# HGRN mixer of a two-block network: two heads on the rows, both directions in the free dimension

## The chip, the cores and the metric

The kernel runs on one core of one Trainium2 chip. The metric is the time of one execution on the device in microseconds; the kernel before takes 1346.8 us (median of 3 runs, 1343.59 to 1347.79). TensorE multiplies matrices, VectorE, ScalarE and GpSimd work elementwise, and SyncE issues most DMAs. The five run side by side and wait for each other by semaphores.

## The reference

The network has a first block (dilated attention, a gated recurrence, cross attention, an MLP) and a second one of two layers, with 256 tokens of 1024 features. Each layer of the second block normalizes, projects into four mixers (latent attention, FNet, differential attention, HGRN2), gates and sums their outputs, and ends with a SwiGLU. The change is in HGRN2, four heads with keys and values of 64 features, run forward and backward:

```python
def forget(z, lb):
    f = lbh + (1.0 - lbh) * sigmoid(z)          # [b, s, head, 64]
    return 1.0 - f, log(f)
k_f, lf_f = forget(f_fwd_in, lb_fwd)
k_b, lf_b = forget(f_bwd_in, lb_bwd)
o_fwd = hgrn2_chunk_scan(q, k_f, v, lf_f)
o_bwd = flip(hgrn2_chunk_scan(flip(q), flip(k_b), flip(v), flip(lf_b)))
o = rmsnorm(o_fwd + o_bwd, g_on) * sigmoid(g_in)
# hgrn2_chunk_scan, per head: out[t] = sum over s <= t of
#   sum_d q[t,d] * exp(lf[s+1..t, d] summed) * k[s,d] * v[s]
```

So each pair of a query and a key has a weight in which every feature is decayed by the gates of all tokens between the two.

## The kernel before

All weights are streamed once, in blocks of 8 tiles of 128 x 128. A block is split into a high part on ScalarE (`_split`, L365, tile `whi`) and a low part on VectorE (L367, `wlo`), and each product of a weight tile with activations is three TensorE instructions, high by high, high by low, low by high (`mm3`, L391 to L393, output `pl`). These products of the layer's input are called the ordinary products here; `lin_t` (L603 to L605) is their form with 512 columns. Mixers are Python generators. `drive` emits one step of each mixer that has started behind each pair of chunks of ordinary products, and a scheduler, with the priorities of `urgent`, then sets the order on each engine. That order is fixed when the program is built; each engine works through its own.

HGRN (`hgrn`, L1342 on) works with a tree over the 256 tokens instead of a scan. The rows of its tiles are 64 features of the forward gates and 64 of the backward gates; heads and tokens lie along the free dimension. `hk` holds keys and `hq` queries, both times decays to the border of the current block; `tot` holds the decay of whole blocks. For each of 7 levels, with blocks of 1, 2, 4 to 64 tokens, the kernel does the following. GpSimd (L1365) writes `qz`, the queries with those rows and halves zeroed that must not meet at this level: the second halves of block pairs stay for forward rows, the first for backward rows. TensorE multiplies the keys of each head and token tile by `qz` (L1371, 8 products, 128 rows, 128 columns, tile `ph`). In fp32 each is two instructions, called passes here. VectorE copies the results into the score matrix `at` where a mask says so (L1374, twice). Then it multiplies the decays into keys (L1383) and queries (L1384) and forms the totals of blocks of twice the size (L1386), each once for the forward and once for the backward rows. The next level's products need these. The diagonal (L1352, `pd`) is computed ahead of the levels, and the products between the two token tiles (L1393, 64 rows) behind them; outputs follow (L1403, L1404).

Other places that are spoken of: dilated attention's scores have 64 rows per head (L1064, `sc`), its outputs 64 columns (L1075); differential attention splits its operands on VectorE, stacks them by DMA (`dks`) and multiplies (L1456, `sd`); sums over partitions for norms are products with 1 to 4 columns (L435).

Of the kernel before, what the change touches and what calls it, by code (L numbers as in the profile page):

```python
# [9 lines left out]
F32 = mybir.dt.float32  # L10
# [9 lines left out]
T = 256  # L20
# [35 lines left out]
def _forget_cols():  # L56
    """Per head the forward and the backward gate's 64 columns."""
    f, b = _cols("hff").reshape(4, 64), _cols("hfb").reshape(4, 64)
    return np.stack([f, b], 1).reshape(-1)


# [6 lines left out]
def plan():  # L68
    """The streamed weights in the order in which they are used: (array, index, columns, kind)."""
# [21 lines left out]
    for l in range(LAYERS):  # L91
        f("w_in_2", (l,), _forget_cols())
# [34 lines left out]
class Cols:  # L127
    """Columns of a [128, n] array, by name."""
# [24 lines left out]
def mla_rows(odd):  # L153
    """Features of a query in the rows of its operand: the plain ones and the rotated ones, those twice."""
    plain = np.arange(64)
    a, b = 64 + np.arange(16), 80 + np.arange(16)
    return np.concatenate([a, b, b, a, plain] if odd else [plain, a, b, b, a])


def params(inp):  # L160
# [27 lines left out]
    lb = np.asarray(inp["hgrn_lb_logits_2"]).reshape(2, 2, 4, 64)  # [dir, layer, head, 64]  # L188
    c.add("lb", lb.transpose(0, 3, 1, 2))                          # [(dir, 64), layer, head]
# [12 lines left out]
def gate_blocks(inp):  # L202
    a = [np.asarray(inp[n])[0].reshape(2, 4, 2, 64, 64) for n in ("rg_a_w", "rg_x_w")]
    a = np.stack(a, 0)                                             # [g, dir, chunk, half, i, j]
    return np.ascontiguousarray(a.transpose(3, 4, 0, 1, 2, 5)).reshape(2, 64, 16, 64)


def constants():
# [17 lines left out]
    c.add("halves", halves())  # L226
# [20 lines left out]
    an = (np.arange(T, dtype=f32)[:, None] * inv2[None]).astype(f32).astype(f8).T      # [16, 256]  # L247
# [10 lines left out]
def masks():  # L258
    """Pairs (key, query) of one 128-token tile whose blocks of 2^l tokens are the halves of one block of 2^(l+1)."""
    s = np.arange(128)  # L260
    m = np.zeros((128, 7, 128))
    for li in range(7):
        b = 1 << li
        m[:, li] = (s[:, None] // (2 * b) == s[None] // (2 * b)) & (s[:, None] // b != s[None] // b)
    return m.reshape(128, 7 * 128)


def halves():
    """For blocks of 2^l: rows of the forward gates keep the second half, rows of the backward gates the first."""
    z = []  # L270
    for li in range(7):
        b = 1 << li
        f = np.concatenate([np.zeros(b), np.ones(b)])
        z.append(np.concatenate([np.tile(f, (64, 1)), np.tile(1 - f, (64, 1))], 0))
    return np.concatenate(z, 1)


# ---------------------------------------------------------------- device
# [5 lines left out]
class Kern:  # L284
    def __init__(self, ctx, tc, a, pcols, ccols, depth=5, ahead=2):
# [18 lines left out]
        # tiles split at a time: first four, later more  # L304
# [9 lines left out]
    # ---- memory  # L314
# [23 lines left out]
    # ---- weight stream  # L338
    def _dma(self):
# [3 lines left out]
        if self.nd < 32 // TB:  # L343
            # the first blocks and the activations take turns
# [43 lines left out]
    # ---- products  # L388
# [6 lines left out]
    def split(self, hi, lo, src, scale=1.0):  # L395
        """hi + lo = src * scale, both with 12 bits or fewer of mantissa."""
# [34 lines left out]
    def token_sums(self, ps, squares):  # L431
        """ps [128, 2, n] += sums over the partitions of squares, a list of ([p, T], indicator [p, n])."""
# [6 lines left out]
class Norm:  # L439
    """Running sum of squares of a [128, 8, T] tensor, two chunks at a time; then 1/rms."""  # L440
# [6 lines left out]
    def square(self, src, scale=None):  # L447
        """Squares of one or two further chunks, src [128, 1 or 2, T]; added behind the next products."""
# [16 lines left out]
    def add(self, sq):  # L465
        """sq [128, 2, T] squares"""
# [10 lines left out]
    def sums(self):  # L477
        """psum [128 tokens, 2] sums of the squares of all features"""
# [19 lines left out]
def interleave(filler, gens):  # L498
    """One step of the filler, then one of each of the others, until all are done."""
# [13 lines left out]
def urgent(tc, gen, offset):  # L513
    """Steps of gen, ahead of what was emitted shortly before."""
# [7 lines left out]
class Body(Kern):  # L522
# [91 lines left out]
    def drive(self, items):  # L614
        """Products in order; behind each pair of chunks one step of every mixer that was started."""
# [1169 lines left out]
```

## Time and profile before

| | us |
|---|---|
| median of 3 runs | 1346.8 |
| lowest, highest | 1343.59, 1347.79 |
| span of the profiled execution, first to last instruction | 1341.6 |
| TensorE busy (PE) | 1291.5 |
| TensorE weight loads busy (PEld) | 1243.3 |
| VectorE busy (DVE) | 929.6 |
| ScalarE busy (ACT) | 639.0 |
| GpSimd busy (POOL) | 258.9 |

The profile is of one execution. Spans of TensorE instructions overlap, since products are pipelined: its pace is read from starts, not from lengths. The granted clock is the share of TensorE's full clock (2.4 GHz) that it was given; 0.5 is 1.2 GHz. Time in which an engine is idle costs something only if a later end depends on it.

### The profile page before, as it was taken

To read this page: it belongs to the slowest core of one execution; us is meant where nothing else is said; L and a number is where in the kernel's file an instruction comes from. 1 tells how busy PE (TensorE), PEld (TensorE's weight loads), DVE (VectorE), ACT (ScalarE), POOL (GpSimd) and SP (SyncE) were. 2 spreads that over 40 slices of the span, in tenths; PEclk is the share of its full clock that TensorE was granted. 3 is DMA by queue.
4 is the path that set the end of the run, shared out by engine and by line. 5 is a ranking of instruction groups with operands and counts; after the bars stand their busy time and mean duration, and the time that the engine had idled before them with its cause. 6 is when DMAs were issued, how large, how long until landed. Compare 5 with 4: busy or idle time off the path is not lost. (4 is left out here: it accounts for less than half of the span.)

```text
span 1341.6 us, 24772 instructions
## 1 busy us (share of the span) xinstructions
PE 1291.5 (96%) x10082; PEld 1243.3 (93%) x10082; DVE 929.6 (69%) x1323; ACT 639.0 (48%) x959; POOL 258.9 (19%) x209
## 2 busy tenths in 40 slices
PE   7979999999999889999999999999899999999998
PEld 6867879999999888999999999998789999999998
DVE  6998547665569996756766666589966577666653
ACT  5556446554444226444554444442364545544432
POOL 8675111000013331222010000113312220100000
PEclk9989999999999999999999999999998999999999
DMA  7533445565674353346556566544532455565562
GB/s 271 175 118 95 141 126 159 187 181 181 188 236 150 119 181 95 94 143 178 183 173 184 180 204 221 183 143 124 173 115 65 142 185 176 176 184 188 178 199 64
DMA packets 68610, 216.64 MB, mean 161 GB/s; under 512 B 10376, under 2 KB 16008, under 8 KB 68496
## 3 DMA queue, kind: packets, MB, share of 16 engines
q1 hardware_dynamic: 68448, 215.02, 51.1%
q8 instruction: 79, 1.29, 0.4%
q14 instruction: 35, 0.29, 0.1%
q0 software_dynamic: 48, 0.03, 0.0%
HBM read 208.73 MB, written 1.05 MB: 156 GB/s over the span
## 5 line engine op out<-in xcount | busy, mean ns | idle before, releaser
L367 DVE TENSOR_TENSOR wlo<-w,whi 128x1024 fp32r<-128x1024 f32 (+1 forms) x381 | 489.5, 1288 | 267.5 <-ACT whi L365 265.3
L365 ACT ACTIVATE whi<-w 128x1024 fp32r<-128x1024 f32 (+1 forms) x386 | 403.6, 1050 | 506.9 <-PE pl L392 256.4
L393 PE MATMUL pl<-xh,wlo 128*128 128x256 f32 x1872 | 535.2, 286 | 10.4 <-POOL wlo L367 6.1
L392 PE MATMUL pl<-xl,whi 128*128 128x256 f32 x1872 | 535.8, 287 | 2.9 <-DVE xl L402 2.9
L391 PE MATMUL pl<-xh,whi 128*128 128x256 f32 x1872 | 535.6, 287 | 2.1 <-DVE ckv L1484 0.9
L393 PEld LDWEIGHTS pl<-xh,wlo 128*128 128x128 f32 x1872 | 362.5, 194 | 13.1 <-POOL wlo L367 6.3
L392 PEld LDWEIGHTS pl<-xl,whi 128*128 128x128 f32 x1872 | 362.6, 194 | 5.6 <-DVE xl L402 3.8
L391 PEld LDWEIGHTS pl<-xh,whi 128*128 128x128 f32 x1872 | 362.2, 194 | 5.2 <-issue 1.8
L472 POOL TENSOR_TENSOR sq<-sq 128x512 f32<-128x512 f32 x24 | 33.9, 1416 | 499.2 <-DVE xl L402 284.3
L391 PE MATMUL pl<-fh,whi 128*128 128x256 f32 x352 | 99.7, 283 | 0.5 <-DVE rs L1733 0.5
L392 PE MATMUL pl<-fl,whi 128*128 128x256 f32 x352 | 99.6, 283 | 0.0
L393 PE MATMUL pl<-fh,wlo 128*128 128x256 f32 x352 | 99.6, 283 | 0.0
L391 PE MATMUL pl<-hdh,whi 128*128 128x256 f32 x256 | 72.5, 283 | 0.6 <-DVE rs L1120 0.6
L392 PE MATMUL pl<-hdl,whi 128*128 128x256 f32 x256 | 72.4, 283 | 0.0
L393 PE MATMUL pl<-hdh,wlo 128*128 128x256 f32 x256 | 72.4, 283 | 0.0
L391 PEld LDWEIGHTS pl<-fh,whi 128*128 128x128 f32 x352 | 67.6, 192 | 0.7 <-DVE rs L1733 0.7
L393 PEld LDWEIGHTS pl<-fh,wlo 128*128 128x128 f32 x352 | 67.6, 192 | 0.0
L392 PEld LDWEIGHTS pl<-fl,whi 128*128 128x128 f32 x352 | 67.6, 192 | 0.0
L663 POOL TENSOR_TENSOR p<-p,rd 128x512 f32<-128x512 f32 x28 | 33.5, 1197 | 119.1 <-DVE rd L656 56.1
L391 PEld LDWEIGHTS pl<-hdh,whi 128*128 128x128 f32 x256 | 49.1, 192 | 0.8 <-issue 0.8
L392 PEld LDWEIGHTS pl<-hdl,whi 128*128 128x128 f32 x256 | 49.1, 192 | 0.0
L393 PEld LDWEIGHTS pl<-hdh,wlo 128*128 128x128 f32 x256 | 49.1, 192 | 0.0
(428 smaller groups left out, 2059.3 us busy)
## 6 DMA issues: line engine op xcount, KB each, us to landing
w<-in_W_dram SPq DMA_DIRECT2D x378, 512.0 KB, 3.6
w<-in_W_dram SPq DMA_DIRECT2D x8, 256.0 KB, 4.5
sw<-in_S_dram SPq DMA_DIRECT2D x4, 512.0 KB, 5.4
h<-in_xT_dram SPq DMA_DIRECT2D x8, 128.0 KB, 4.2
mem<-in_memT_dram SPq DMA_DIRECT2D x2, 512.0 KB, 5.8
sw<-qe SPq DMA_DIRECT2D x16, 64.0 KB, 3.2
dt<-in_C_dram SPq DMA_DIRECT2D x4, 256.0 KB, 7.1
dqs<-dhi SPq DMA_DIRECT2D x16, 64.0 KB, 3.5
```

Source lines behind the costliest of these rows:

```text
L365: self.nc.scalar.activation(hi, w, AF.Copy)
L367: eng.tensor_tensor(lo, w, hi.bitcast(F32), op=OP.subtract)
L391: mm(out, wh, xh, start=first, stop=False, skip_group_check=shared)
L392: mm(out, wh, xl, start=False, stop=False, skip_group_check=shared)
L393: mm(out, wl, xh, start=False, stop=last, skip_group_check=shared)
L472: self.eng.tensor_tensor(self.acc, self.acc, sq, op=OP.add)
L663: self.nc.gpsimd.tensor_tensor(p, p, r.rearrange("p (q o) -> p q o", o=1).to_broadcast([128, 2, T]), op=OP.mult)
```

## The change

The rows of the HGRN tiles are now 64 features of one head and 64 of another, and the four places along the free dimension are the two directions of the two head pairs. So the forget gates are projected in two parts, forward and backward, each directly in the layout of its columns; queries come out of their projection in the layout in which they are used, and are one tile of half the size. At each level the products are made per direction, per head and per token tile: 16 instead of 8 products, with 64 rows instead of 128, and with only those 64 queries that meet keys at this level, so that nothing has to be zeroed. The two heads are alternated in the innermost loop and write to two PSUM banks. The masked copies are four instead of two, each for half of the queries. A level's key decays, query decays and totals are one VectorE instruction each, over both directions and all rows, by access patterns written out in `view`. The diagonal takes the sum of forward and backward keys (`ks`). The constant `halves` is gone, and comments are dropped.

```diff
 def plan():
-        f("w_in_2", (l,), _forget_cols())
+        f("w_in_2", (l,), _cols("hff"))
+        f("w_in_2", (l,), _cols("hfb"))
...
 def params(inp):
-    lb = np.asarray(inp["hgrn_lb_logits_2"]).reshape(2, 2, 4, 64)  # [dir, layer, head, 64]
-    c.add("lb", lb.transpose(0, 3, 1, 2))                          # [(dir, 64), layer, head]
+    lb = np.asarray(inp["hgrn_lb_logits_2"]).reshape(2, 2, 2, 2, 64)
+    c.add("lb", lb.transpose(3, 4, 1, 0, 2))
...
 def constants():
-    c.add("halves", halves())
...
 def masks():
-    s = np.arange(128)
-    m = np.zeros((128, 7, 128))
+    s, t = np.arange(128)[:, None], np.arange(128)
+    m = np.zeros((128, 2, 7, 64))
     for li in range(7):
         b = 1 << li
-        m[:, li] = (s[:, None] // (2 * b) == s[None] // (2 * b)) & (s[:, None] // b != s[None] // b)
-    return m.reshape(128, 7 * 128)
+        for z in range(2):
+            q = t[(t // b) % 2 == 1 - z][None]
+            m[:, z, li] = (s // (2 * b) == q // (2 * b)) & ((s // b) % 2 == z)
+    return m.reshape(128, 2 * 7 * 64)
...
-        q0 = self.g4("q0")
+        q0 = self.h2("q0")
...
         def c_hq(j, ps, n):
-            for r in range(2):
-                for par in range(2):
-                    V.tensor_tensor(q0[64 * r:64 * r + 64, par::2], ps[64 * par:64 * par + 64],
-                                    rx["b"][64 * par:64 * par + 64].rearrange("p (o t) -> p o t", o=1)
-                                    .to_broadcast([64, 2, T]), op=OP.mult)
+            V.tensor_tensor(q0, ps, self.bT(rx["b"]), op=OP.mult)
...
         def hgrn():
             ad, ao = at
-            V.tensor_tensor(hq, q0, fz, op=OP.mult)
+            rows = [slice(0, 64), slice(64, 128)]
+            tile = [slice(0, 128), slice(128, 256)]
+            ks = self.h2("ks")
+            V.tensor_tensor(ks, hk[:, 0:2], hk[:, 2:4], op=OP.add)
+            pairs = lambda a: a.rearrange("p (z c) t -> p z (c t)", z=2)
+            V.tensor_tensor(pairs(hq), q0.rearrange("p (o c) t -> p o (c t)", o=1).to_broadcast([128, 2, 512]),
+                            pairs(fz), op=OP.mult)
             yield
+            pd = [self.ps("pd").rearrange("p (k t) -> p k t", k=4) for _ in range(2)]
+            for k in range(4):
+                for p in range(2):
+                    nc.tensor.matmul(pd[p][:, k], ks[rows[p], k // 2, tile[k % 2]], q0[rows[p], k // 2, tile[k % 2]],
+                                     start=True, stop=True)
...
             for li in range(7):
                 B = 1 << li
-                nb = 512 // B                     # pairs of blocks over the heads
-                qz = self.g4("qz")
-                zm = hz[:, 2 * B - 2:4 * B - 2].rearrange("p (o b) -> p o b", o=1).to_broadcast([128, nb, 2 * B])
-                nc.gpsimd.tensor_tensor(qz.rearrange("p h (n b) -> p (h n) b", b=2 * B),
-                                        hq.rearrange("p h (n b) -> p (h n) b", b=2 * B), zm, op=OP.mult)
-                for hp in range(2):
-                    ps = self.ps("ph").rearrange("p (k t) -> p k t", k=4)
-                    for k in range(4):
-                        s = slice((k % 2) * 128, (k % 2) * 128 + 128)
-                        nc.tensor.matmul(ps[:, k], hk[:, 2 * hp + k // 2, s], qz[:, 2 * hp + k // 2, s],
-                                         start=True, stop=True)
-                    m = self.mk[:, li * 128:li * 128 + 128].rearrange("p (o t) -> p o t", o=1)
-                    V.copy_predicated(ad[:, 4 * hp:4 * hp + 4], m.to_broadcast([128, 4, 128]), ps)
-                # decays to blocks of twice the size
-                for z in range(2):
-                    r = slice(64 * z, 64 * z + 64)
-                    tt = tot[z].rearrange("p (n s) -> p n s", s=2)
-                    far, near = tt[:, :, z], tt[:, :, 1 - z]
-                    kh = hk[r].rearrange("p h (n s b) -> p (h n) s b", s=2, b=B)[:, :, z]
-                    qh = hq[r].rearrange("p h (n s b) -> p (h n) s b", s=2, b=B)[:, :, 1 - z]
-                    ex = lambda a: a.rearrange("p (n o) -> p n o", o=1).to_broadcast([64, nb, B])
-                    V.tensor_tensor(kh, kh, ex(near), op=OP.mult)
-                    V.tensor_tensor(qh, qh, ex(far), op=OP.mult)
-                    nt = tots[li % 2][r, :nb]
-                    V.tensor_tensor(nt, far, near, op=OP.mult)
-                    tot[z] = nt
+                nb = 256 // B
+                ps = [self.ps("ph").rearrange("p (z k t) -> p z k t", z=2, k=4) for _ in range(2)]
+                for k in range(4):
+                    c, kt = divmod(k, 2)
+                    for z in range(2):
+                        for p in range(2):
+                            q = hq[rows[p], 2 * z + c, tile[kt]].rearrange("p (n s b) -> p n s b", s=2, b=B)
+                            nc.tensor.matmul(ps[p][:, z, k].rearrange("p (n b) -> p n b", b=B),
+                                             hk[rows[p], 2 * z + c, tile[kt]], q[:, :, 1 - z], start=True, stop=True)
+                for p in range(2):
+                    o = ad[:, 4 * p:4 * p + 4].rearrange("p k (n s b) -> p k n s b", s=2, b=B)
+                    for z in range(2):
+                        m = mk[:, z:z + 1, li].rearrange("p o (n b) -> p o n b", b=B)
+                        V.copy_predicated(o[:, :, :, 1 - z], m.to_broadcast([128, 4, 64 // B, B]),
+                                          ps[p][:, z].rearrange("p k (n b) -> p k n b", b=B))
+                def view(a, o, d, *rest):
+                    return bass.AP(tensor=a.tensor, offset=a.offset + o, ap=[list(a.ap[0]), [d, 2], *rest])
+                first = lambda a: view(a, 0, 512 + B, [2 * B, nb], [1, B])
+                second = lambda a: view(a, B, 512 - B, [2 * B, nb], [1, B])
+                kh, qh = first(hk), second(hq)
+                V.tensor_tensor(kh, kh, view(tot, 1, 2 * nb - 1, [2, nb], [0, B]), op=OP.mult)
+                V.tensor_tensor(qh, qh, view(tot, 0, 2 * nb + 1, [2, nb], [0, B]), op=OP.mult)
+                if li < 6:
+                    tt = tot.rearrange("p (n s) -> p n s", s=2)
+                    nt = tots[li % 2][:, :2 * nb]
+                    V.tensor_tensor(nt, tt[:, :, 0], tt[:, :, 1], op=OP.mult)
+                    tot = nt
                 yield
...
         items = [
-            self.lin(k2, L, 4, x, c_forget), self.lin_t(k2, L, 256, x, c_fx), ...
+            self.lin(k2, L, 2, x, c_forget(0)), self.lin(k2, L, 2, x, c_forget(1)), self.lin_t(k2, L, 256, x, c_fx), ...
```


The order that the scheduler makes of it is known ahead of a run. On TensorE, the products of level 0 in the first of the two layers stood before as one block (`pl` is the ordinary product, `ph` the level's):

```order
L392 MATMUL pl_4814<-xl_84,whi_4778 128x256
L393 MATMUL pl_4814<-xh_83,wlo_4779 128x256
L1371 MATMUL ph_4959<-qz_4957,hk_4411 128x128 x4
L1371 MATMUL ph_4965<-qz_4957,hk_4411 128x128 x4
L391 MATMUL pl_4814<-xh_83,whi_4778 128x256
```

Now the same place begins so, and goes on in this alternation for all 16:

```order
L379 MATMUL pl_4813<-xl_84,whi_4745 128x256
L1360 MATMUL ph_4956<-hq_4412,hk_4411 128x64
L380 MATMUL pl_4813<-xh_83,wlo_4746 128x256
L1360 MATMUL ph_4957<-hq_4412,hk_4411 128x64
L378 MATMUL pl_4813<-xh_83,whi_4745 128x256
```

Each level product has moved between two ordinary products; the second layer has the same pattern. Levels 1 to 6 stand as blocks of 16, alternating the two banks, except that in levels 2 and 4 of both layers 8 or fewer products of another mixer stand ahead of the last one.

On VectorE, the same level stood so before, from the query decays of level 0 on (`wlo` is a weight split, `hgt` and `dqe` are evacuations):

```order
L1384 TENSOR_TENSOR hq_4412<-hq_4412,fz_4410 64x512 x2
L367 TENSOR_TENSOR wlo_4899<-w_4746,whi_4898 128x1024
L1374 COPY_PREDICATED at0_4416<-mk_82,ph_4959 128x512
L1374 COPY_PREDICATED at0_4416<-mk_82,ph_4965 128x512
L1383 TENSOR_TENSOR hk_4411<-hk_4411,fz_4410 64x512 x2
L1307 TENSOR_TENSOR dqe_4420<-pl_4814,n45b_4578 128x512
L1384 TENSOR_TENSOR hq_4412<-hq_4412,tot0_4418 64x256x2 x2
```

Now:

```order
L1324 TENSOR_TENSOR hgt_4414<-pl_4742,n45b_4578 128x512
L1366 COPY_PREDICATED at0_4416<-mk_82,ph_4956 128x256 x2
L1366 COPY_PREDICATED at0_4416<-mk_82,ph_4957 128x256 x2
L1376 TENSOR_TENSOR hk_4411<-hk_4411,fz_4410 128x2x256
L1377 TENSOR_TENSOR hq_4412<-hq_4412,fz_4410 128x2x256
L354 TENSOR_TENSOR wlo_4898<-w_4743,whi_4897 128x1024
L1294 TENSOR_TENSOR dqe_4420<-pl_4813,n45b_4578 128x512
L354 TENSOR_TENSOR wlo_4928<-w_4773,whi_4927 128x1024
```

The four copies, keys and queries follow each other directly, and the weight split that stood between them has moved behind.

## Rows read from the trace of the kernel before

**Rows 1.** The page, part 1: each engine's busy time and instructions.
```profile
PE 1291.5 (96%) x10082; PEld 1243.3 (93%) x10082; DVE 929.6 (69%) x1323; ACT 639.0 (48%) x959; POOL 258.9 (19%) x209
```

**Rows 2.** Windows of HGRN; columns: window, length, PE, PEld, DVE, ACT, POOL, clock, DMA.
```profile
427.60:515.00 87.40, 79.92 (x600) 76.42 (x598) 84.99 (x121) 31.65 (x48) 29.93 (x12) 0.96 0.49 151
...
895.50:983.00 87.50, 80.08 (x598) 76.56 (x598) 84.23 (x118) 32.80 (x48) 30.44 (x12) 0.96 0.47 145
```

**Rows 3.** Waits of TensorE, 400 to 1020 us: total, times, longest.
```profile
PE ph L1371 <- DVE hk L1383: 7.1, 5, 2.2
...
PE sd L1456 <- DMA dks<-dlo: 4.4, 2, 2.3
```

**Rows 4.** Groups by line, level work: busy, mean ns, idle before.
```profile
L1365 POOL TENSOR_TENSOR qz<-hq,ct 128x1024 f32<-128x1024 f32 x14 | 38.3, 2733 | 52.9 <-DVE hq L1384 37.0 <-DVE hq L1345 7.7 <-DVE tot L1386 4.7
...
L1374 DVE COPY_PREDICATED at<-mk,ph 128x512 f32<-128x512 uint8 x28 | 19.5, 730 | 0.1
...
L1383 DVE TENSOR_TENSOR hk<-hk,tot 64x512 f32<-64x512 f32 x24 | 21.6, 901 | 0.3
...
L1384 DVE TENSOR_TENSOR hq<-hq,tot 64x512 f32<-64x512 f32 x24 | 16.4, 682 | 0.4
...
L1386 DVE TENSOR_TENSOR tot<-tot 64x256 f32<-64x256 f32 (+5 forms) x24 | 7.4, 307 | 0.4
```

**Rows 5.** Timeline of GpSimd and VectorE: start, length, instruction.
```profile
445.58 3.20 POOL L1365 TENSOR_TENSOR qz<-hq,ct 128x1024 f32<-128x1024 f32 x1 [3.45 <-PE ph L1371]
...
446.61 3.25 DVE L367 TENSOR_TENSOR wlo<-w,whi 128x1024 fp32r<-128x1024 f32 x1
...
466.67 1.22 DVE L367 TENSOR_TENSOR wlo<-w,whi 128x1024 fp32r<-128x1024 f32 x1
```

**Rows 6.** Timeline of TensorE around a block of level products.
```profile
465.42 0.28 PE L391 MATMUL pl<-xh,whi 128*128 128x256 f32 x1
...
465.54 1.95 PE L1371 MATMUL ph<-qz,hk 128*128 128x128 f32 x16
...
467.44 0.28 PE L393 MATMUL pl<-xh,wlo 128*128 128x256 f32 x1
```

**Rows 7.** Timeline of TensorE, products with 4 columns, latent attention.
```profile
539.52 1.85 PE L435 MATMUL mst<-ct,sqq 128*128 128x4 f32 x16
...
541.23 0.59 PE L435 MATMUL mst<-ct,sq 128*128 128x4 f32 x4
...
541.74 0.38 PE L435 MATMUL mst<-ct,skv 32*128 32x4 f32 x2
...
542.05 0.39 PE L435 MATMUL mst<-ct,sq 128*128 128x4 f32 x2
```

**Rows 8.** Timeline of TensorE, half-row scores of dilated attention, block 1.
```profile
87.70 1.14 PE L1064 MATMUL sc<-kr,qr 64*128 64x256 f32 x8
...
107.62 1.13 PE L1064 MATMUL sc<-kr,qr 64*128 64x256 f32 x4
...
108.68 0.39 PE L392 MATMUL pl<-ml,whi 128*128 128x256 f32 x1
...
108.90 0.28 PE L393 MATMUL pl<-mh,wlo 128*128 128x256 f32 x1
```

**Rows 9.** Timeline of TensorE, into the half-row cross-tile products.
```profile
980.92 0.28 PE L392 MATMUL pl<-xl,whi 128*128 128x256 f32 x1
...
981.13 1.71 PE L1393 MATMUL ph<-hq,hk 64*128 64x128 f32 x16
```

**Rows 10.** Timeline of TensorE, one full product between two narrow ones.
```profile
115.27 0.38 PE L393 MATMUL pl<-mh,wlo 128*128 128x256 f32 x1
...
115.58 0.65 PE L1075 MATMUL po<-pts,vv 128*64 128x256 f32 x2
```

**Rows 11.** Windows after HGRN, layer one: narrow products, then what follows.
```profile
538.50:544.10 5.60, 5.60 (x42) 4.99 (x42) 2.57 (x11) 2.55 (x5) 2.23 (x2) 1.00 0.13 50
...
544.10:547.50 3.40, 3.40 (x16) 3.00 (x15) 0.90 (x2) 1.09 (x2) 2.64 (x2) 0.50 0.00 0
```

More of the change, by code (lines that the diff above doesn't have):

```diff
@@ L53, in _cols @@
     return np.arange(o, o + w)
-def _forget_cols():
-    f, b = _cols("hff").reshape(4, 64), _cols("hfb").reshape(4, 64)
-    return np.stack([f, b], 1).reshape(-1)
 def _krope_cols():
@@ L258, in masks @@
 def masks():
-    s = np.arange(128)
-    m = np.zeros((128, 7, 128))
+    s, t = np.arange(128)[:, None], np.arange(128)
+    m = np.zeros((128, 2, 7, 64))
     for li in range(7):
         b = 1 << li
-        m[:, li] = (s[:, None] // (2 * b) == s[None] // (2 * b)) & (s[:, None] // b != s[None] // b)
-    return m.reshape(128, 7 * 128)
[L268 to L275, printed above, removed]
+        for z in range(2):
+            q = t[(t // b) % 2 == 1 - z][None]
+            m[:, z, li] = (s // (2 * b) == q // (2 * b)) & ((s // b) % 2 == z)
+    return m.reshape(128, 2 * 7 * 64)
 def bc(ap, shape):
@@ L1319, in layer, with c_forget, f @@
         tots = [self.sp.tile([128, 512 >> i], F32, name=f"tot{i}", tag=f"tot{i}", bufs=1) for i in range(2)]
-        def c_forget(k, ps, n):
-            t = self.h2("zt")
-            V.tensor_tensor(t, ps, self.bT(rx["b"]), op=OP.mult)
-            nc.scalar.activation(t, t, AF.Tanh, scale=0.5)
-            for c in range(2):
-                i = k + c
-                a, b = self.cA[:, l, i:i + 1], self.cB[:, l, i:i + 1]
-                V.tensor_scalar(fz[:, i], t[:, c], b, a, op0=OP.mult, op1=OP.add)
-                V.tensor_scalar(hk[:, i], t[:, c], self.cN[:, l, i:i + 1], b, op0=OP.mult, op1=OP.add)
-        def c_hq(j, ps, n):
-            for r in range(2):
-                for par in range(2):
-                    V.tensor_tensor(q0[64 * r:64 * r + 64, par::2], ps[64 * par:64 * par + 64],
-                                    rx["b"][64 * par:64 * par + 64].rearrange("p (o t) -> p o t", o=1)
-                                    .to_broadcast([64, 2, T]), op=OP.mult)
+        def c_forget(z):
+            def f(k, ps, n):
+                t = self.h2("zt")
+                V.tensor_tensor(t, ps, self.bT(rx["b"]), op=OP.mult)
+                nc.scalar.activation(t, t, AF.Tanh, scale=0.5)
+                for c in range(2):
+                    i = 2 * z + c
+                    a, b = self.cA[:, l, i:i + 1], self.cB[:, l, i:i + 1]
+                    V.tensor_scalar(fz[:, i], t[:, c], b, a, op0=OP.mult, op1=OP.add)
+                    V.tensor_scalar(hk[:, i], t[:, c], self.cN[:, l, i:i + 1], b, op0=OP.mult, op1=OP.add)
+            return f
+        def c_hq(j, ps, n):
+            V.tensor_tensor(q0, ps, self.bT(rx["b"]), op=OP.mult)
         def c_hg(j, ps, n):
@@ L1344, in hgrn @@
             ad, ao = at
[L1345 to L1352 removed]
+            rows = [slice(0, 64), slice(64, 128)]
[5 more added lines that the diff above has]
+                            pairs(fz), op=OP.mult)
+            yield
+            pd = [self.ps("pd").rearrange("p (k t) -> p k t", k=4) for _ in range(2)]
+            for k in range(4):
+                for p in range(2):
+                    nc.tensor.matmul(pd[p][:, k], ks[rows[p], k // 2, tile[k % 2]], q0[rows[p], k // 2, tile[k % 2]],
                                      start=True, stop=True)
[L1354 removed]
+            for p in range(2):
+                V.tensor_tensor(ad[:, 4 * p:4 * p + 4], pd[p],
                                 self.C("ident").rearrange("p (o t) -> p o t", o=1).to_broadcast([128, 4, 128]),
@@ L1357, in hgrn @@
             yield
[L1358 to L1359 removed]
+            tot = fz.rearrange("p h t -> p (h t)")
+            mk = self.mk.rearrange("p (z l t) -> p z l t", z=2, l=7)
             for li in range(7):
                 B = 1 << li
[L1362 to L1388 removed]
@@ L1389, in hgrn @@
-            for z in range(2):
-                r = slice(64 * z, 64 * z + 64)
-                ps = self.ps("ph").rearrange("p (h t) -> p h t", h=4)
-                for hd in range(4):
-                    nc.tensor.matmul(ps[:, hd], hk[r, hd, z * 128:z * 128 + 128],
-                                     hq[r, hd, (1 - z) * 128:(2 - z) * 128], start=True, stop=True)
-                nc.scalar.activation(ao[:, z::2], ps, AF.Copy)
+                nb = 256 // B
+                ps = [self.ps("ph").rearrange("p (z k t) -> p z k t", z=2, k=4) for _ in range(2)]
@@ new lines, in hgrn @@
+                for k in range(4):
[5 more added lines that the diff above has]
+                                             hk[rows[p], 2 * z + c, tile[kt]], q[:, :, 1 - z], start=True, stop=True)
+                for p in range(2):
+                    o = ad[:, 4 * p:4 * p + 4].rearrange("p k (n s b) -> p k n s b", s=2, b=B)
[3 more added lines that the diff above has]
+                                          ps[p][:, z].rearrange("p k (n b) -> p k n b", b=B))
@@ new lines, in hgrn @@
+                if li < 6:
[3 more added lines that the diff above has]
+                    tot = nt
+                yield
+            ps = [self.ps("ph").rearrange("p (k t) -> p k t", k=4) for _ in range(2)]
+            for k in range(4):
+                c, z = divmod(k, 2)
+                for p in range(2):
+                    nc.tensor.matmul(ps[p][:, k], hk[rows[p], 2 * z + c, tile[z]], hq[rows[p], 2 * z + c, tile[1 - z]],
+                                     start=True, stop=True)
@@ L1396, in hgrn @@
+            for p in range(2):
+                nc.scalar.activation(ao[:, 4 * p:4 * p + 4], ps[p], AF.Copy)
             yield
             po = self.ps("poh").rearrange("p (c t) -> p c t", c=2)
-            for hd in range(4):
-                par, c = hd % 2, hd // 2
+            for c in range(2):
                 for qt in range(2):
-                    o = po[64 * par:64 * par + 64, c, qt * 128:qt * 128 + 128]
-                    w = lambda st: vh[:, st, hd * 64:hd * 64 + 64]
-                    nc.tensor.matmul(o, w(qt), ad[:, 2 * hd + qt], start=True, stop=False)
-                    nc.tensor.matmul(o, w(1 - qt), ao[:, 2 * hd + 1 - qt], start=False, stop=True)
+                    for i, a in enumerate((ad, ao)):
+                        st = 1 - qt if i else qt
+                        for p in range(2):
+                            hd = 2 * c + p
+                            nc.tensor.matmul(po[rows[p], c, tile[qt]], vh[:, st, hd * 64:hd * 64 + 64],
+                                             a[:, 4 * p + 2 * c + st], start=i == 0, stop=i == 1)
@@ L1660, in layer @@
         mixers = {n: urgent(self.tc, m, HM) for n, m in ((3, hgrn()), (2, diff()), (0, mla()), (1, fnet()))}
-        items = [self.lin(k2, L, 4, x, c_forget), self.lin_t(k2, L, 256, x, c_fx), ("start", mixers[1]), self.lin(k2, L, 2, x, c_hq), ("start", mixers[3]),
+        items = [self.lin(k2, L, 2, x, c_forget(0)), self.lin(k2, L, 2, x, c_forget(1)), self.lin_t(k2, L, 256, x, c_fx), ("start", mixers[1]), self.lin(k2, L, 2, x, c_hq), ("start", mixers[3]),
                  self.lin(k2, L, 2, x, c_hg), self.lin(k2, L, 2, x, scaled(dqe)), self.lin(k2, L, 2, x, scaled(dke)),
```

8 lines of the change are left out of this document (removed).

## The prediction

> **What bounds the kernel now.** I read the page's busy times first: TensorE is busy 96% of the 1341.6 us, VectorE 69%, GpSimd 19% [rows 1]. So what VectorE and GpSimd do counts only where TensorE waits for them, and what TensorE does counts nearly everywhere. The windows of the two HGRN stretches show a place where it waits [rows 2]: in 87.4 and 87.5 us VectorE is busy 84.99 and 84.23, while TensorE is idle for 7.5 and 7.4 us and its mean granted clock is 0.96. The missing 4% of both stretches are another 7.0 us. So 21.9 us are lost there, the most that faster operands could return. The waits name them [rows 3]: the level products wait for the decayed keys (7.1 us in 5 waits), and the scores of differential attention for a DMA of operands that VectorE splits first (4.4 us in 2).
>
> VectorE is full there for two reasons. One is its level work: per level 2 copies, 2 products on keys, 2 on queries, 2 totals [rows 4]. The other is GpSimd: while it zeroes queries for 3.20 us from 445.58, a weight split that takes 1.22 us at 466.67 takes 3.25 us and ends just after the GpSimd instruction [rows 5]. There are 14 of these, 2.73 us each [rows 4].
>
> **The change part by part.** *VectorE and GpSimd.* Before, a level costs VectorE 2 x 0.73 for copies, 2 x 0.90 for keys, 2 x 0.68 for queries and 2 x 0.31 for totals, 5.2 us [rows 4]. After, it has 4 copies of half the length and one of each other kind, on 128 rows instead of 64. A half-length copy is not in the trace: it lies between 0.37 us (half) and 0.73 (all of it fixed); I take 0.45, nearer to the half because the 0.31 mean of the totals shows short instructions to be cheap. A level is then 4 x 0.45 + 2 x 0.68 + 0.3 = 3.5 us, and 14 levels save 24 us. The query evacuations go from 8 to 2 and the sums of keys add 2, priced as the query products at 0.68: 2.7 us saved. The delays behind GpSimd's 38.3 us go as well. VectorE's 97% of the stretches should fall to some 80%. This reaches TensorE's time through the 21.9 us alone. The chain from one level's products to the next (copies, keys, queries) takes 3.2 us and lies beside the 34 to 41 other products of 0.12 us that the new order puts between levels, 4.1 to 4.9 us; the key waits should go. The DMA of the split operands stays close behind; I leave half of its 4.4 us and one half-clock stretch of 1.7 us. Returned: 21.9 - 2.2 - 1.7 = **18 us**, between 0 and 21.9.
>
> *A block of level products.* Before, 8 products of 128 rows and 128 columns, two passes each, run as one block: from 465.42 to 467.44 are 2.02 us for the block and two ordinary products of 0.12, so 1.78 us, 0.111 per pass [rows 6]. After, 16 products of 64 rows and 64 columns make 32 passes. Fewer columns do not shorten a pass: 16 passes with 4 columns take from 539.52 to 541.23, 0.107 each [rows 7]. But two row halves run side by side: eight half-row passes of dilated attention took 1.14 us, where four of one half took 1.13 [rows 8]. The new loop alternates the halves, so 16 pairs at 0.111 are 1.78 us again, no gain and no loss. (The Trainium skill, "TensorEngine Tiling (Array Packing)", Theoretical Speedup, gives up to 2x where the contraction is 64 long. By that a level would take 0.9 us and 14 levels 12 us less; the 4-column passes speak against it.)
>
> *Into half rows and out.* An ordinary product is followed 0.12 us later by the next, but 0.21 us later by the half-row block at 981.13 [rows 9]. Four half-row passes of 256 columns last 1.06 us to the next product at 108.68, against 0.89 for full-row ones (an estimate: twice the 0.111 of 128 columns, four times [rows 6]), and that product is followed after 0.22 instead of 0.12 [rows 8]. Together 0.09 + 0.17 + 0.10 = 0.36 us for one excursion. (The Trainium skill, "TensorEngine Tiling (Array Packing)", Key Properties, says that a change of the tiling mode drains TensorE, and names no time; it speaks against this change, and the trace agrees.)
>
> Levels 1 to 6 of two layers stay blocks: 12 x 0.36 = +4.3 us. In levels 2 and 4 the scheduler puts other products ahead of the last half, so that it stands alone: 4 x 0.5, +2.0. The diagonal's 16 passes become 8 pairs, 0.89 + 0.36 against 1.78, -0.5 a layer; the cross-tile products save as much in the second layer, where they stay together: -1.5. The output products only alternate their column halves; taken at 0, between -1 and +1.
>
> *Level 0.* Here the order is another: each of the 16 half-row products stands alone between two ordinary ones, in both layers. No pair can form, and the engine changes over 32 times. One period: a product behind one excursion and ahead of the next took 0.31 us (115.27 to 115.58) [rows 10]; two passes on few rows with 4 columns, until full rows go on, took 0.31 (541.74 to 542.05) [rows 7], and 64 columns add some 0.05 (an estimate, a quarter of the 0.22 for 256). That is 0.67 us; 16 of them are 10.7, minus the 16 ordinary products (1.9) and the old block (1.8): +7.0 a layer, **+14 us**. Bounds: +1.8 a layer if only the passes count (16 x (0.12 + 0.22) - 3.7), +7.5 if the block's 0.36 is added to each.
>
> *The clock.* It fell where products were narrow although TensorE had no gap: in the 5.6 us from 538.5, mostly products of 1 to 4 columns, it was busy throughout, and then the grant was 0.50 for 3.4 us [rows 11]. Level 0 is 10.7 us of lone narrow products and change-overs. If the clock falls 5.5 us after its start, as there, the other 5.2 us take twice as long: +5.2 a layer, **+10.4 us**; bounds 0 and 8 (2 us earlier, and another 1.7 until it rises).
>
> *The start.* The constants lose 254 columns and the scheduler reorders parts of block 1: 0, within 4 us either way (the three runs shown differ by 4.2).
>
> The sum: -18 + 4.3 + 2.0 - 1.5 + 14 + 10.4 = +11.2 us on the profiled execution. Its span of 1341.6 lies 5.2 us under the median of 1346.8; the change is added to the median: **1358 us**.
>
> **Rivals.** *The clock holds in level 0.* Other half stretches followed idle time, and lone products leave some activity. The sum is then +0.8, 1348 us: inside 0.3% or 4 us, about what this measurement can tell from no change. Against it: rows 11 had no idle time either.
>
> *Lone half-row products cost their passes alone,* and the clock has no cause to fall: -18 + 2 x 1.8 + 4.8 = -9.6, 1337 us, faster. For it: the halves do load beside each other [rows 8]. Against it: an ordinary product holds all rows, and rows 8 to 10 show the gap at each change.
>
> *A pass of half the rows and 64 columns takes half of 0.111.* Then a level's 16 pairs take 0.9 us, 14 levels give 12 us back on the forecast, and it comes to 1346 us, no change. Against it: the 4-column passes [rows 7]. (It is what the table of the Trainium skill, "TensorEngine Tiling (Array Packing)", Theoretical Speedup, would give.)
>
> *VectorE stays late.* With half-length copies at 0.73 a level takes 4.6 us and its chain 4.3, at the edge of the 4.1 to 4.9 that cover it; with half of the 18 us still lost, 1367 us.
>
> **How the numbers follow.** The forecast has 0.58, the holding clock 0.15, lone products at their passes 0.18, the half pass 0.04, late VectorE 0.05. The forecast is slower except with a lucky start (0.56 slower, 0.02 same). The holding clock is same but for the start's 4 us (0.04 slower, 0.08 same, 0.03 faster); lone products at their passes are faster (0.17) or same (0.01); the half pass gives 0.02 same, 0.02 faster; late VectorE is slower. Together 0.65 slower, 0.13 same, 0.22 faster. The forecast's own range is 1348 (clock holding in one layer, a lucky start) to 1369. The whole range starts at 1333, where the cheap case returns all 21.9 us instead of 18, and leaves out about 0.08 there and 0.08 above 1369.
>
> **What would show it.** In the changed kernel's profile: level 0's half-row products at a period of 0.6 to 0.75 us, and a grant of 0.5 before they end; blocks of 32 passes in about 2.2 us; VectorE near 80% in the HGRN stretches, no wait of TensorE for decayed keys over 1 us. The forecast is wrong if level 0 takes under 6 us with its 16 ordinary products, or if TensorE still idles 7 us a layer.

## The result and the profile after

The changed kernel takes 1358.7 us (median of 4 runs, 1357.22 to 1363.99) against 1346.7: 1.0102 times the time before, with a 95% interval of 1.0083 to 1.0120. It is 12 us slower; the forecast was 1358.

The profiled execution is the slowest of the four (1363.99, span 1362.2, mean granted clock 0.971; the other three have 0.975 to 0.979), and the profiled execution of the kernel before, by its span of 1341.6, is that kernel's fastest (1343.59). So the terms between the two profiles add up to more than the medians show. The page's busy times [rows 1]:

```profile
PE 1323.0 (97%) x10306; PEld 1264.5 (93%) x10306; DVE 887.4 (65%) x1303; ACT 637.2 (47%) x957; POOL 221.7 (16%) x195
```

VectorE lost 42 us and GpSimd 37, and TensorE, the bound, gained 32. The windows, with the columns of [rows 2], are the two HGRN stretches and then level 0 of each layer:

```profile
427.80:513.30 85.50, 82.16 (x589) 72.71 (x587) 56.35 (x108) 26.85 (x44) 12.36 (x9) 0.86 0.38 113
910.00:996.00 86.00, 86.00 (x636) 77.00 (x635) 59.45 (x112) 30.41 (x48) 12.64 (x9) 0.86 0.42 125
431.30:446.00 14.70, 14.70 (x51) 10.51 (x51) 5.08 (x9) 1.83 (x3) 0.00 (x0) 0.68 0.23 71
915.10:930.90 15.80, 15.80 (x50) 11.07 (x48) 3.71 (x6) 1.27 (x3) 0.00 (x0) 0.59 0.22 67
```

VectorE is at 66 and 69% instead of 97, TensorE's idle time is nearly gone, and yet the granted clock fell from 0.96 to 0.86. In level 0 TensorE is busy throughout and its clock is 0.68 and 0.59. The timeline of TensorE shows level 0, first at 2.4 GHz, then at 1.2.

```profile
431.13 0.28 PE L379 MATMUL pl<-xl,whi 128*128 128x256 f32 x1
431.35 0.43 PE L1360 MATMUL ph<-hq,hk 64*128 64x64 f32 x2
431.71 0.39 PE L380 MATMUL pl<-xh,wlo 128*128 128x256 f32 x1
432.02 0.43 PE L1360 MATMUL ph<-hq,hk 64*128 64x64 f32 x2
...
437.95 0.69 PE L1360 MATMUL ph<-hq,hk 64*128 64x64 f32 x2
438.57 0.58 PE L380 MATMUL pl<-xh,wlo 128*128 128x256 f32 x1
439.08 0.69 PE L1360 MATMUL ph<-hq,hk 64*128 64x64 f32 x2
```

From one half-row product to the next are 0.67 us (431.35 to 432.02), then 1.13 (437.95 to 439.08). A closed block, level 1, beside [rows 6]:

```profile
452.38 0.28 PE L378 MATMUL pl<-xh,whi 128*128 128x256 f32 x1
452.59 2.00 PE L1360 MATMUL ph<-hq,hk 64*128 64x64 f32 x32
454.52 0.39 PE L379 MATMUL pl<-xl,whi 128*128 128x256 f32 x1
454.75 0.28 PE L380 MATMUL pl<-xh,wlo 128*128 128x256 f32 x1
```

From the ordinary product ahead of it to the second one behind it are 2.37 us (452.38 to 454.75). Without the two ordinary products of 0.12 that is 2.13, against 1.78 before. Of the waits in [rows 3] neither is left; one of 3.2 us is there in their place:

```profile
PE ph L1360 <- DVE tot L1381: 3.2, 1, 3.2
PE sm L1574 <- DVE kp L1566: 1.8, 1, 1.8
```

VectorE's level work, all levels of both layers but the first keys and queries [rows 4]:

```profile
L1366 DVE COPY_PREDICATED at<-mk,ph 128x256 f32<-128x256 uint8 x56 | 24.4, 529 | 28.6 <-PE ph L1360 28.6
...
L1376 DVE TENSOR_TENSOR hk<-hk,tot 128x512 f32<-128x512 f32 x12 | 8.2, 687 | 0.0
L1377 DVE TENSOR_TENSOR hq<-hq,tot 128x512 f32<-128x512 f32 x12 | 8.2, 680 | 0.0
```

A half-length copy costs 24.4 / 56 = 0.44 us of busy time (0.45 was taken; by the same measure a full-length one cost 19.5 / 28 = 0.70). Queries cost half of what they did (8.2 against 16.4), keys less than half (8.2 against 21.6).

The difference lies in the two mixer stages: before from 411.2 to 687.1 and from 877.2 to 1158.1, after from 411.6 to 701.9 and from 892.1 to 1179.2 (from a layer's first norm product, `n45p` or `nxp`, to `n6p`, the next one behind the mixers). Outside of them both kernels take 784.8 us. I split each stage into TensorE's idle time, half the length of its stretches at 1.2 GHz (what the clock took), and the rest, which is the pace of its instructions. Half is a convention, and a little too much: an ordinary product takes 0.21 us at 1.2 GHz (two from 464.29 to 464.72, in lines further below) where it takes 0.12 at 2.4. Both layers together, in us, in the profiled execution of each kernel of this study:

| kernel | mixer stages | idle | clock | pace |
|---|---|---|---|---|
| before | 556.9 | 18.3 | 11.9 | 526.7 |
| after | 577.4 | 8.4 | 27.4 | 541.6 |
| e1_blocks | 556.8 | 16.5 | 15.3 | 525.0 |
| e2_fullrow0 | 553.0 | 9.9 | 8.5 | 534.6 |
| e4_unpaired | 570.1 | 4.6 | 18.7 | 546.8 |
| e5_before_noqz | 541.2 | 7.6 | 8.5 | 525.1 |
| e6_twohead_tiles | 533.7 | 3.8 | 6.8 | 523.1 |
| e7_gp_back_before | 556.1 | 18.7 | 11.9 | 525.5 |
| e8_gp_back_after | 583.1 | 12.9 | 27.4 | 542.8 |

### The profile page after: what moved, and what is told of

It is laid out like the page before. It is cut to its first block, busy times and chain, and to the rows that moved or that the text cites. A ratio compares the mean times of both kernels' runs of the same rounds, so it can differ in the third digit from the quotient of the medians.

```text
span 1362.2 us, 25170 instructions
## 1 busy us (share of the span) xinstructions
PE 1323.0 (97%) x10306; PEld 1264.5 (93%) x10306; DVE 887.4 (65%) x1303; ACT 637.2 (47%) x957; POOL 221.7 (16%) x195
## 5 line engine op out<-in xcount | busy, mean ns | idle before, releaser
L354 DVE TENSOR_TENSOR wlo<-w,whi 128x1024 fp32r<-128x1024 f32 (+1 forms) x381 | 475.9, 1252 | 283.5 <-ACT whi L352 280.0
L380 PE MATMUL pl<-xh,wlo 128*128 128x256 f32 x1872 | 542.6, 290 | 13.0 <-DVE wlo L354 7.5
L379 PE MATMUL pl<-xl,whi 128*128 128x256 f32 x1872 | 542.3, 290 | 3.0 <-DVE xl L389 2.9
L380 PEld LDWEIGHTS pl<-xh,wlo 128*128 128x128 f32 x1872 | 367.3, 196 | 18.4 <-DVE wlo L354 8.2
L379 PEld LDWEIGHTS pl<-xl,whi 128*128 128x128 f32 x1872 | 367.2, 196 | 8.0 <-DVE xl L389 4.2
L378 PEld LDWEIGHTS pl<-xh,whi 128*128 128x128 f32 x1872 | 366.9, 196 | 5.4 <-issue 2.7
```

What stands on the lines that cost most here:

```text
L354: eng.tensor_tensor(lo, w, hi.bitcast(F32), op=OP.subtract)
L378: mm(out, wh, xh, start=first, stop=False, skip_group_check=shared)
L379: mm(out, wh, xl, start=False, stop=False, skip_group_check=shared)
L380: mm(out, wl, xh, start=False, stop=last, skip_group_check=shared)
```

## Experiments

Ratios and intervals here are against executions of the kernel before that were taken beside the experiments (median 1344.1 us, for e6 to e8 1345.0), not against the 1346.7 above.

**e1_blocks: no alternation.** The products of all levels and of the diagonal get a higher priority, so that each level is a closed block.

```diff
+                with self.tc.high_priority(400):
                     for k in range(4):
                         c, kt = divmod(k, 2)
```

> Theory (the loss is the alternation at level 0, which the clock then doubles): with all level products and the diagonal in closed blocks, level 0 takes one block of about 2.1 us instead of 16 periods of 0.675, 6.7 us a layer less; the four lone halves go (about 2 us); the half-clock stretch of 14 to 17 us behind level 0 goes too (some 10 us over both layers). Together about -25 us on 1358.7: 1333 us, 1327 to 1340. Rival A (narrow half-row products bring the clock down wherever they stand): only the pace comes back, 1343. Rival B (the alternation hid VectorE's chain; closed blocks make TensorE wait for decayed keys again): idle of 7 us a layer, 1347 or more.

Measured: 1341.7 us, 0.9980 of before (0.9962 to 0.9997): 17 less than the changed kernel, and just above the range. Pace came back as expected (541.6 to 525.0), and the clock's term by 12.1 (27.4 to 15.3) where some 10 were expected, so rival A falls. But the idle time doubled, and that is rival B in part. The waits:

```profile
PE ph L1362 <- DVE hq L1379: 5.4, 3, 3.9
PE sd L1455 <- DMA dks<-dlo: 4.3, 2, 2.8
```

The longest, 3.9 us, is not VectorE's own work. Its timeline shows that it sat idle 2.94 us for a DMA that exchanges rows for differential attention, with a level's copies queued behind:

```profile
928.21 0.69 DVE L1425 TENSOR_TENSOR sw<-sw,dt 128x512 f32<-128x512 f32 x1 [2.94 <-DMA sw<-dke]
928.82 0.68 DVE L1426 TENSOR_TENSOR dke<-dke,dt 128x512 f32<-128x512 f32 x1
929.42 1.41 DVE L1368 COPY_PREDICATED at<-mk,ph 128x256 f32<-128x256 uint8 x4
```

**e2_fullrow0: the same order, full rows.** In level 0 alone, hk and hq are read with all 128 rows.

```diff
-                            q = hq[rows[p], 2 * z + c, tile[kt]].rearrange("p (n s b) -> p n s b", s=2, b=B)
+                            q = hq[rows[p] if li else slice(0, 128), 2 * z + c, tile[kt]].rearrange("p (n s b) -> p n s b", s=2, b=B)
-                                             hk[rows[p], 2 * z + c, tile[kt]], q[:, :, 1 - z], start=True, stop=True)
+                                             hk[rows[p] if li else slice(0, 128), 2 * z + c, tile[kt]], q[:, :, 1 - z], start=True, stop=True)
```

> Level 0's 16 products take all 128 rows (both heads are summed, so that level's scores are not the reference's); the order on every engine is that of the changed kernel. Theory (it is the change between row halves and full rows): a period falls from 0.675 us to 0.12 + 0.22 = 0.34, 5.4 us a layer, and with half the length of narrow work the clock stretch shrinks to one or none: 1338 us, 1333 to 1346. Rival (any lone fp32 product of 64 columns between ordinary ones costs this): period stays above 0.6, 1356 to 1361.

Measured: 1340.4 us, inside the range: 18.2 less than the changed kernel, which is more than its whole loss (0.9974 of before, 0.9960 to 0.9988). The timeline of TensorE in level 0:

```profile
432.31 0.34 PE L1360 MATMUL ph<-hq,hk 128*128 128x64 f32 x2
432.45 0.36 PE L380 MATMUL pl<-xh,wlo 128*128 128x256 f32 x1
432.66 0.33 PE L1360 MATMUL ph<-hq,hk 128*128 128x64 f32 x2
```

and its window in each layer (columns as before; the clock is the third from the right):

```profile
431.50:437.70 6.20, 6.20 (x56) 6.20 (x56) 4.37 (x6) 1.63 (x3) 0.00 (x0) 1.00 0.54 153
902.60:908.20 5.60, 5.60 (x51) 5.60 (x50) 3.12 (x5) 1.01 (x3) 0.00 (x0) 1.00 0.57 176
```

The period is 0.35 us (432.31 to 432.66) and the clock stays whole. The order of every engine is that of the changed kernel, so the change-over between row halves and full rows is shown as the cause: half of level 0's period, and with it the clock. Whether the clock fell for the change-overs themselves, or because with them the narrow products last twice as long, this run does not separate.

**e4_unpaired: halves one after the other.** As e1_blocks, with the loop over the two heads outermost.

```diff
-                    for k in range(4):
-                        c, kt = divmod(k, 2)
-                        for z in range(2):
-                            for p in range(2):
+                    for p in range(2):
+                        for k in range(4):
+                            c, kt = divmod(k, 2)
+                            for z in range(2):
```

> As e1_blocks, but all products of one row half before those of the other. Theory (halves run side by side only when neighbours alternate): a block takes 32 x 0.11 = 3.5 us instead of 1.93, 14 levels +22 us over e1_blocks: about 1355, and the clock may fall behind some of the blocks, up to 10 more. Rival (a half-row pass takes half of 0.11 by itself): blocks stay at 1.9 us, the time that of e1_blocks.

Measured: 1356.3 us, 14.5 more than e1_blocks; the pace alone grew by the expected 22 (525.0 to 546.8). Against that the idle time fell by 11.9 (16.5 to 4.6), and the clock took 3.4 more. No wait of a level product is left: the longer blocks cover VectorE's chain. A block, on TensorE:

```profile
912.29 0.28 PE L380 MATMUL pl<-xh,wlo 128*128 128x256 f32 x1
912.50 3.39 PE L1362 MATMUL ph<-hq,hk 64*128 64x64 f32 x32
915.82 0.38 PE L378 MATMUL pl<-xh,whi 128*128 128x256 f32 x1
```

It takes 3.32 us to the next product instead of 1.93: 32 passes of 0.104, where alternating neighbours ran in pairs. (The Trainium skill, "TensorEngine Tiling (Array Packing)", Theoretical Speedup, promises up to 2x for contractions of 64 rows. The trace gives 1.72x, 3.32 / 1.93, but only against the same half-row passes: 8 full-row products do the same work in 1.71, see e6. That factor is in the forecast's 1.78 us already, by its pairs; the 0.9 us that the prediction worked out with it counts it twice.)

**e5_before_noqz: GpSimd's work taken away.** The kernel before, whose products read the queries without the zeroing.

```diff
-                qz = self.g4("qz")
...
-                nc.gpsimd.tensor_tensor(qz.rearrange("p h (n b) -> p (h n) b", b=2 * B),
-                                        hq.rearrange("p h (n b) -> p (h n) b", b=2 * B), zm, op=OP.mult)
+                qz = hq
```

> The kernel before without GpSimd's zeroed queries: the products read the queries as they are, so pairs that shouldn't meet are added. Theory (GpSimd's instructions were half of what made VectorE late): VectorE's weight splits in the HGRN stretches fall from 1.46 us to 1.22, TensorE's idle from 7.4 us a layer to under 3, one or two half-clock stretches go: 1339 us, 1333 to 1345. The scheduler alternates level 0's eight full-row products of the second layer with ordinary ones: by the first theory that costs their passes alone, 0.34 us a period. Rival (VectorE's own instruction count was what counted): idle stays near 6 us a layer, 1346.

Measured: 1324.0 us, 0.9852 of before (0.9837 to 0.9867): 20 us less, more than twice the 8 that the theory expected, and outside its range. VectorE still executes every one of its instructions of before, and the two stretches' windows show it at 91%:

```profile
427.00:515.00 88.00, 86.88 (x673) 82.83 (x672) 80.27 (x140) 37.10 (x62) 12.64 (x8) 0.98 0.53 156
887.00:972.00 85.00, 83.56 (x655) 80.17 (x654) 77.32 (x133) 37.57 (x57) 13.56 (x8) 1.00 0.52 162
```

So VectorE's own instruction count was not, by itself, what made TensorE wait. In layer 2 the scheduler alternated eight full-row products of level 0 with ordinary ones, at 0.34 us a period like e2.

**e7_gp_back_before: which side of GpSimd?** e5 and, per level, a GpSimd product that nothing reads:

```diff
+                gd = self.g4("gd")
+                nc.gpsimd.tensor_tensor(gd.rearrange("p h t -> p (h t)"), dt.rearrange("p h t -> p (h t)"),
+                                        tots[li % 2][:, :1].to_broadcast([128, 1024]), op=OP.mult)
```

> e5_before_noqz with a GpSimd product of 128x1024 per level whose result nothing reads, started by the level's totals. Theory (GpSimd slows VectorE while both run): weight splits are delayed again, mean over 1.35 us, and TensorE's idle comes back in part: 1337 us, 1331 to 1346. Rival (what cost the time was the products' wait for GpSimd's result, the longer chain): 1324, within 3 us of e5_before_noqz.

Measured: 1342.3 us, inside the range. An unread result costs 18 us, and the mixers' idle time is back (7.6 to 18.7). (The scheduler's order is not quite that of e5, but TensorE's pace is the same in the table.) The groups of the first HGRN stretch, GpSimd's product and VectorE's weight split:

```profile
L1386 POOL TENSOR_TENSOR gd<-dt,tot 128x1024 f32<-128x1024 f32 x7 | 15.6, 2231 | 43.8 <-DVE tot L1383 43.8
```
```profile
L367 DVE TENSOR_TENSOR wlo<-w,whi 128x1024 fp32r<-128x1024 f32 x22 | 34.1, 1554 | 0.1
```

In e5 the split takes 1.218 us in that stretch; in the second HGRN stretch of e7 it takes 1.350. No VectorE instruction of the first stretch waits for `gd`: the delay is inside VectorE's instructions. The rival falls: products that wait for nothing of GpSimd's are as late as before. (The Trainium skill, "SBUF — State Buffer", Who interferes with whom, says that a VectorE instruction with two inputs in SBUF contends with a GpSimd instruction that reads SBUF, and that the lock on the ports they share is exclusive. The trace agrees, here by the mean and in [rows 5] by the split of 3.25 us: it ended 1.08 us after GpSimd's instruction, not just after it as the prediction says, so most of its own 1.22 us came once GpSimd was done.)

**e8_gp_back_after: the same product in the changed kernel.** The expectation says levels 0 to 5, but the lines stand in the loop of all 7 levels, and the trace has 14 of these products, as in e7.

```diff
+                gd = self.g4("gd")
+                nc.gpsimd.tensor_tensor(gd.rearrange("p h t -> p (h t)"), dt.rearrange("p h t -> p (h t)"),
+                                        tot[:, :1].to_broadcast([128, 1024]), op=OP.mult)
```

> The changed kernel with the same unread GpSimd product in levels 0 to 5. Theory (with one instruction per decay step VectorE, at 66% of these stretches, has room for the delay): TensorE's idle grows by less than 3 us a layer: 1362 us, 1357 to 1366. Rival (it was GpSimd's going alone that returned the idle time, VectorE's fewer instructions are worth nothing): the idle time of before comes back, 5 to 7 us a layer: 1370.

Measured: 1369.4 us (1365.21 to 1377.34), 1.0189 of before (1.0158 to 1.0220), above the theory's range. The idle time grew as the theory said, by 2.9 and 1.6 us in the layers, and VectorE rose by 9.6 us in the first stretch:

```profile
427.50:516.00 88.50, 82.21 (x594) 72.18 (x594) 65.99 (x109) 27.90 (x45) 28.91 (x16) 0.88 0.37 112
```

The time is the rival's all the same. By the two profiled executions it is 5.8 us (1369.76 and 1363.99), nearly all in the table's idle and pace; the other 5 between the medians I did not place. By the idle column either remedy alone goes with part of it (e8 from 18.3 to 12.9, e5 to 7.6), but in e8 only in the second layer (9.0 to 3.9; 9.3 to 9.0 in the first), beside a TensorE that is slower there than before.

**e6_twohead_tiles: the two prices avoided.** Rows, gates and keys of the changed kernel; one query tile per direction holds each head's rows in its own columns and zeros elsewhere, written once a layer, so that one full-row product serves both heads.

```diff
+        hq = [self.g4(f"hq{z}").rearrange("p (h c) t -> p h c t", h=2) for z in range(2)]
...
+                    nc.scalar.activation(hq[z][r, 1 - p], fz[r, 2 * z:2 * z + 2], AF.Copy, scale=0.0)
+                    V.tensor_tensor(hq[z][r, p], q0[r], fz[r, 2 * z:2 * z + 2], op=OP.mult)
...
+                        q = hq[z][:, :, c, tile[kt]].rearrange("p h (n s b) -> p h n s b", s=2, b=B)
+                        nc.tensor.matmul(ps[z][:, :, k].rearrange("p h (n b) -> p h n b", b=B),
+                                         hk[:, 2 * z + c, tile[kt]], q[:, :, :, 1 - z], start=True, stop=True)
```

> A version from both: rows, gates and key decays of the changed kernel, but queries are kept in two tiles (one for each direction) with zeros for the other head, written once a layer by ScalarE, so that a level is again 8 products of 128 rows and 128 columns and GpSimd has nothing to do; query decays are two VectorE instructions of 512 elements, copies two of 512. Theory (half rows and GpSimd were the two prices): blocks cost 1.71 us and 0.08 as before, TensorE's idle stays under 3 us a layer as in e5_before_noqz, the diagonal saves 0.6 a layer: 1322 us, 1317 to 1329. Rival (the strided queries slow the products, or VectorE with 3.8 us a level is late again): 1335 or more.

Measured: 1318.3 us (1312.52 to 1319.72), 0.9788 of before (0.9767 to 0.9810), inside the range. It beats both kernels. The windows of the HGRN stretches and a level's block:

```profile
426.00:512.00 86.00, 86.00 (x677) 81.90 (x676) 75.72 (x130) 39.34 (x69) 14.12 (x10) 1.00 0.48 154
884.00:970.00 86.00, 86.00 (x670) 81.37 (x670) 75.78 (x132) 42.28 (x74) 15.52 (x11) 1.00 0.48 154
```
```profile
443.97 0.28 PE L380 MATMUL pl<-xh,wlo 128*128 128x256 f32 x1
444.09 1.95 PE L1361 MATMUL ph<-hq,hk 128*128 128x128 f32 x16
445.80 0.36 PE L378 MATMUL pl<-xh,whi 128*128 128x256 f32 x1
```

TensorE is busy throughout both stretches at a whole clock, and a block takes 1.71 us as before.

## Why the prediction was right, point by point

The direction and the size came out (+11.2 forecast, +11.9 by the medians), and the step that decides, the change-overs at level 0, is shown by e2. That the medians agree within 1 us is in part luck: not every term came out. By the profiled executions, 20.6 us apart in span:

| term | forecast | measured |
|---|---|---|
| TensorE's idle time | -12.7 (14.9 less 2.2 left) | -9.9 |
| clock: old stretches and new | -5.3 + 10.4 = +5.1 | +15.5 |
| pace: level 0, blocks, lone halves, diagonal | 14 + 4.3 + 2.0 - 1.5 = +18.8 | +14.9 |

A mean granted clock of 0.971 over 1362.2 us is 39.5 us lost to the clock, in the whole program; the other three executions, at 0.975 to 0.979, lost 28 to 34. If all of that difference lies in the mixer stages, the clock's term in them is 5 to 11 us smaller than the 15.5 of this one, nearer to the forecast; no profile shows in which stage it lies.

*Level 0's period* was the best of the steps: 0.67 forecast, 0.675 measured (seven periods, 431.35 to 436.08), and e2 shows that it is the change-over that costs, not the 64 columns.

*A closed block* was to cost 0.36 more; it costs 2.13 - 1.78 = 0.35. Pairs form only by alternation (e4).

*The clock* fell in level 0 of both layers, as forecast, 5.3 us after the start in the first (436.62, forecast 5.5) and 2.7 us after it in the second (917.90). It stayed low for 13.7 and 17.1 us, until some microseconds after the last lone half-row product; that is 6.8 and 8.5 us a layer where 5.2 was taken. A pair of products did not take twice as long at 1.2 GHz as assumed, but 1.13 / 0.675 = 1.67 times, so part of what the forecast put under the clock and the pace of level 0 isn't there: over the 20 periods at 1.2 GHz that is 20 x (0.675 - 1.13 / 2) = 2.2 of the 3.9 us by which the pace is below its term.

*The old half-clock stretches* are the step that failed: "one half-clock stretch of 1.7 us" was to be left in the HGRN stretches, and beside level 0's there are three: 3.4 us from 463.93 and 6.8 from 474.17 in the first layer, 6.8 from 948.62 in the second, 8.5 us by the convention of the table. The one from 474.17 begins 1.2 us behind the wait of 3.2 us; the other two came with TensorE busy, around the last half of level 2, which stands alone behind 16 passes with 4 columns; in the first layer:

```profile
461.68 1.95 PE L422 MATMUL dst<-ct,sq 128*128 128x4 f32 x16
463.56 0.43 PE L1360 MATMUL ph<-hq,hk 64*128 64x64 f32 x2
463.92 0.58 PE L379 MATMUL pl<-xl,whi 128*128 128x256 f32 x1
464.29 0.41 PE L380 MATMUL pl<-xh,wlo 128*128 128x256 f32 x1
464.51 0.41 PE L378 MATMUL pl<-xh,whi 128*128 128x256 f32 x1
464.72 0.41 PE L379 MATMUL pl<-xl,whi 128*128 128x256 f32 x1
```

It is not the lone half alone: in e1, whose level 2 is a closed block, the clock falls in the same place (455.80, behind the block and 14 passes with 4 columns). The forecast had priced the lone halves (4 x 0.5 us), but no clock behind such narrow runs.

*The idle time* returned nearly as forecast, for a reason that was priced wrongly. I gave VectorE's 24 us of saved instructions the first place and named GpSimd's delays beside them. e5 returns as much with VectorE's work untouched. Yet e1, with the changed kernel's work on VectorE and GpSimd at the pace of before, has 16.5 us idle, only 1.8 less than before, and e6 at that pace 3.8. So what the two remedies return depends on the order too, and how much of it the slower TensorE hid in the changed kernel the runs do not separate. VectorE's load, forecast near 80%, came to 66 and 69%: in the first stretch the split fell from 1.46 to 1.22 us as GpSimd's work went, and only 14 splits fall into it, before 22. And "no wait of TensorE for decayed keys over 1 us" did not hold: the one of 3.2 us is VectorE waiting for the exchange DMA, with level 2's last copies, its keys and its queries behind it in the queue:

```profile
464.57 0.69 DVE L387 TENSOR_TENSOR dlo<-dqe,dhi 128x512 fp32r<-128x512 f32 x1
468.88 0.69 DVE L1423 TENSOR_TENSOR sw<-sw,dt 128x512 f32<-128x512 f32 x1 [3.61 <-DMA sw<-dke]
...
470.17 0.74 DVE L1366 COPY_PREDICATED at<-mk,ph 128x256 f32<-128x256 uint8 x2
470.83 0.68 DVE L1376 TENSOR_TENSOR hk<-hk,tot 128x512 f32<-128x512 f32 x1
```

*The start* cost nothing: the first mixer stage begins 0.4 us later.

Of the rivals, the holding clock (1348) and lone products at their passes (1337) are ruled out by the level 0 rows, the pass of half length by the blocks of 1.93 us, late VectorE by its 66 and 69%.

## What to carry to other kernels

Where the bound is TensorE, count the change-overs between half-row and full-row products before counting products: a lone half-row product between ordinary ones costs two and a half times its passes here (0.675 less 0.12, against 2 x 0.11), and a run of 16 took the clock too. Where an engine is full and another one runs beside it, take the second one's work away in an experiment before making the first one's shorter: the delay may come from that second engine. Zeros that stay in place let a full-row product serve two heads without a change-over and without anybody zeroing per step.

## What the runs showed of the hardware beyond that

A GpSimd product of 128x1024 whose result nothing reads, 14 times 2.3 us, made the kernel 18 us slower (e7 against e5), though GpSimd was idle for two thirds of these stretches. TensorE's clock can halve while the trace shows no idle time of it: level 0's windows have it busy for 14.7 of 14.7 us at a clock of 0.68. And executions of one kernel differ by some us together with the mean granted clock: of 19 executions of the kernel before, beside e1 to e5, the fastest took 1341.5 us at 0.988, the slowest 1348.7 at 0.980.
